# Small matmuls in another order, and pairs of feature tiles computed together, in a two-layer RWKV-7 / mLSTM trunk

## The chip, the cores and the metric

One core of one Trainium2 chip runs the whole program. The metric is the device time of one execution in microseconds (us); of several runs the median is taken. A profiled execution gives the rows shown below. TensorE is PE in these rows (PEld: its weight loads), VectorE is DVE, ScalarE is ACT, GpSimd is POOL, SyncE is SP.

## The reference, cut to what matters

Layer 0 mixes time with RWKV-7, layer 1 with a chunkwise mLSTM; each is followed by a SwiGLU FFN. Width 1024, 1024 frames, float32.

```python
r, wl, k, v, al, gl = outs                      # projections of token-shifted mixes
w_log = -softplus(-(w0 + tanh(wl) @ w2)) - 0.5  # "lora" of the decay; a = sigmoid(a0 + al @ a2)
state = state * w_t + (state @ a_t) b_t + v_t k_t   # per head 64 x 64, one step per frame
y = state @ r_t
...
w_intra = exp(d_log - m_t) * einsum('bhctd,bhcsd->bhcts', q, k)   # mLSTM scores
x = x + g1 * (mixed @ w_out);  x = x + g2 * swiglu(...)
```

## The kernel before, in words

Features lie on the partitions, frames on the free axis, in two halves (`hf`) of 512 frames. A **wide product** (`rkv` for r, k and v, `project` for w_out) makes eight feature tiles of 128 x 512. `dense` (line 244) makes one: for each of eight blocks `kt` of the input three matmuls, high weights by high input, high by low, low by high, all in one PSUM bank, 24 matmuls a tile. The weights of a tile come through `weights` (line 237): a load, an ACT copy to the high part (line 211) and a DVE subtraction to the low part (line 212). In the stage of the chunks (below) the tags `whi` and `wlo` have two buffers each and the PSUM tag `dn` two banks; where `self.deep` is set, c1 and c2 serve as well. `spill` (line 418) evicts a bank on ACT and stores it. The input parts come from `mixed` (line 403) into the 18 buffers of tag `a`.

The RWKV recurrence is solved in chunks of 64 frames. Each of 16 rounds (a pair of heads times a half) passes through four steps, one behind the other in a pipeline over the rounds (`chunks`, line 1450): `rw_prep` (masked score matrices), `rw_inverse` (inverse of a triangular 64 x 64 matrix per chunk and head, from 16 x 16 blocks up), `rw_solve`, and `rw_chain` with `rw_finish` (the state, chunk by chunk). Between the steps `run` lets a generator of **fillers** go on by a quota: the products v of the first half, the gate, the loras and k, r, v of the second half, the first out-projection. This is "the stage of the chunks" in what follows.

In `rw_inverse` (line 657) the first two groups of small matmuls are 16 x 16: 8 in each of four partition quadrants, quadrant after quadrant, with `tile_position=(32 * q, 32 * q)` (lines 697 to 709). The last groups are 32 x 32: for each end `e` of the partitions eight matmuls into bank `iv`, an ACT copy, eight more, another copy, and then the same for the other `e` (lines 719 to 729). In `rw_solve` (line 731) two groups of 16 matmuls of 64 x 64 go chunk by chunk, two heads in a row on the same partitions (lines 754 to 765), and a third goes through bank `tr` for one `e` and then the other (lines 769 to 776). A float32 matmul of these stands as two MATMUL instructions in the trace: 32 matmuls are 64 there. `ml_prep` (line 1284) forms the scores of two heads, four matmuls each over 64 partitions, head after head in two banks.

`lora` (line 428) ends with eight tiles of two matmuls: the first over 128 partitions (`st` holds the high weights on partitions 0 to 63 and the low ones on 64 to 127; `th` and `tl` are twice the same 64 rows), the second over partitions 0 to 63 alone (line 449).

The order on each engine is made by a planner from priorities and a model of times; a matmul that waits holds up those behind it on its engine. `ahead` raises the priority of a block.

Of the kernel before, what the change touches and what calls it, by code (L numbers as in the profile page):

```python
# [17 lines left out]
P = 128  # L18
D = 1024
T = 1024  # L20
KT = 8
# [108 lines left out]
class K:  # L130
# [113 lines left out]
    def dense(self, ps, w, xs, m=P):  # L244
# [3 lines left out]
        for kt, (xh, xl) in enumerate(xs):  # L248
# [2 lines left out]
            self.mm(ps, hi[:, c], xl, start=False, stop=False)  # L251
            self.mm(ps, lo[:, c], xh, start=False, stop=kt == n - 1)


    def ada_prep(self):
        nc = self.nc
# [171 lines left out]
    def lora(self, hf, arr, xs=None):  # L428


        nc, A = self.nc, self.A
        first, second, bias, seg, func = {"s": ("lw", "w2", "w0", 1, AF.Tanh), "a": ("la", "a2", "a0", 4, AF.Copy)}[arr]
        xs = xs or self.mixed(seg)
        ps = self.bank("dn")
        self.dense(ps, self.weights(A[first]), xs)
        yield 5
        t = self.t("tmp")
        nc.scalar.activation(t, ps, func)
        th, tl = self.a0()
        self.split(th, tl, t)  # L440
        raw, hi, st = self.wtiles(A[second])
        nc.scalar.activation(hi, raw, AF.Copy)
        nc.scalar.activation(st[0:64], raw[0:64], AF.Copy)
        nc.vector.tensor_tensor(st[64:128], raw[64:128], hi[64:128].bitcast(F32), SUB)
        for j in range(KT):
            c = slice(j * P, j * P + P)
            ps = self.bank("dn")
            self.mm(ps, st[:, c], th, start=True, stop=False)
            self.mm(ps, hi[0:64, c], tl[0:64], start=False, stop=True)
            self.spill(arr, j, hf, ps, AF.Sigmoid, bias=self.col(bias, j))  # L450
            if hf == 0 or j % 4 == 3:
                yield 2
# [37 lines left out]
    def rkv(self, hf, arr, xs=None):  # L490
        nc = self.nc
        seg, w = {"r": (0, "wr"), "k": (2, "wk"), "v": (3, "wv")}[arr]
        xs = xs or self.mixed(seg)
        if arr == "k":
            ss = self.t("ss", [16, HT])
        held = None

        def sums(j, sq):
            nonlocal p2
            if hf == 1 or j == 0:  # L500
                p2 = self.bank("iv" if hf == 0 else ("sc", "iv")[j % 2])
            sel = self.k_("hsel")[:, 14 - 2 * j:30 - 2 * j]
            if hf == 0:
                self.mm(p2[0:16], sel, sq, start=j == 0, stop=j == KT - 1)
            else:
                self.mm(p2[0:16], sel, sq)
            if j == 0 and hf == 1 or j == KT - 1 and hf == 0:
                nc.vector.tensor_copy(ss, p2[0:16])
            elif hf == 1:
                nc.vector.tensor_tensor(ss, ss, p2[0:16], ADD)  # L510

        p2 = None
        for j in range(KT):
            wt = self.early.pop(0) if self.early else self.weights(self.A[w][j])
            ps = self.bank("dn")
            self.dense(ps, wt, xs)
            if held:
                sums(*held)
            self.spill(arr, j, hf, ps)
            if arr == "k":  # L520
                sq = self.t("tmp")
                nc.scalar.activation(sq, ps, AF.Square, scale=self.col("k_k", j))
                held = j, sq
                if j == KT - 1:
                    sums(*held)
            if arr == "k" and j == KT - 1:
                self.kk_norm(ss, hf)
            self.done[arr, hf] = j + 1
            yield 6 if arr == "k" else 5

    def kk_norm(self, ss, hf):

# [124 lines left out]
    def rw_inverse(self, S):  # L657
# [36 lines left out]
        nc.vector.transpose(XN, XD)  # L694
        Y1 = self.t("Y1", [P, 8, 32])
        ps = self.bank("iv", [P, 8, 16])
        for q in range(4):
            r, e = slice(32 * q, 32 * q + 16), 0 if q >= 2 else 1
            o = 32 * (q % 2) + 16
            for c in range(8):  # L700
                self.mm(ps[r, c, :], SA[r, e, c, o:o + 16], XN[r, c, 0:16], tile_position=(32 * q, 32 * q))
        for q in range(4):
            r = slice(32 * q, 32 * q + 16)
            nc.scalar.activation(Y1[r, :, 0:16], ps[r], AF.Copy)
        ps = self.bank("iv", [P, 8, 16])
        for q in range(4):
            r = slice(32 * q, 32 * q + 16)
            for c in range(8):
                self.mm(ps[r, c, :], Y1[r, c, 0:16], XB[r, c, :], tile_position=(32 * q, 32 * q))
        for q in range(4):  # L710
            r = slice(32 * q, 32 * q + 16)
# [4 lines left out]
            o = 32 * (q % 2)  # L716
            nc.scalar.activation(SA[r, e, :, o:o + 32], XD[r], AF.Copy)
        Y1 = self.t("Y1", [P, 8, 32])
        for e in range(2):
            o = 0 if e else 64  # L720
            r0, r1 = slice(o, o + 32), slice(o + 32, o + 64)
            ps = self.bank("iv", [P, 8, 32])
            for c in range(8):
                self.mm(ps[r1, c, :], SA[r0, e, c, 32:64], XN[r0, c, :], tile_position=(o, o + 32))
            nc.scalar.activation(Y1[r1], ps[r1], AF.Copy)
            ps = self.bank("iv", [P, 8, 32])
            for c in range(8):
                self.mm(ps[r0, c, :], Y1[r1, c, :], XD[r1, c, :], tile_position=(o + 32, o))
            nc.scalar.activation(SA[r0, e, :, 32:64], ps[r0], AF.Copy)

    def rw_solve(self, S):

        nc = self.nc
        AR, SA = S["AR"], S["SA"]
        v = self.rload("v", S["j"], S["hf"])
        VU = self.t("VU", [P, 8, P])
        ps = self.bank("tr")
        for u in range(4):
            nc.tensor.transpose(ps[:, u * P:u * P + P], v[:, u * P:u * P + P], self.k_("ident"))
        p3 = ps.rearrange("p (u f) -> p u f", f=P)  # L740
        nc.scalar.activation(VU[0:64, 0::2, :], p3[0:64], AF.Copy)
        nc.scalar.activation(VU[64:128, 1::2, :], p3[64:128], AF.Copy)
        AT = self.t("AT", [P, 4, P])
        ps = self.bank("tr")
        fl = AR.rearrange("p c t -> p (c t)")
        for u in range(4):
            o = 2 * u * P + 64
            nc.tensor.transpose(ps[:, u * P:u * P + P], fl[:, o:o + P], self.k_("ident"))
        p3 = ps.rearrange("p (u f) -> p u f", f=P)
        nc.scalar.activation(AT[64:128], p3[0:64], AF.Copy)  # L750
        nc.scalar.activation(AT[0:64], p3[64:128], AF.Copy)
        Z = self.t("Z", [P, 4, P])
        ps = self.bank("px")
        for c in range(8):
            vr, ur = self.rows(c)
            for h in range(2):
                o = (c // 2) * P + 64 * h
                self.mm(ps[ur, o:o + 64], SA[vr, c % 2, 2 * (c // 2) + h, :], VU[vr, c, 64 * h:64 * h + 64])
        nc.scalar.activation(Z, ps.rearrange("p (u f) -> p u f", f=P), AF.Copy)
        ps = self.bank("px")  # L760
        for c in range(8):
            vr, ur = self.rows(c)
            for h in range(2):
                o = (c // 2) * P + 64 * h
                self.mm(ps[ur, o:o + 64], SA[ur, c % 2, 2 * (c // 2) + h, :], Z[ur, c // 2, 64 * h:64 * h + 64])
        p3 = ps.rearrange("p (u f) -> p u f", f=P)
        nc.scalar.activation(VU[64:128, 0::2, :], p3[64:128], AF.Copy)
        nc.scalar.activation(VU[0:64, 1::2, :], p3[0:64], AF.Copy)
        for e in range(2):
            ps = self.bank("tr", [P, 4, 64])  # L770
            ur = self.rows(e)[1]
            for u in range(4):
                for h in range(2):
                    hs = slice(64 * h, 64 * h + 64)
                    self.mm(ps[hs, u, :], AT[ur, u, hs], SA[ur, e, 2 * u + h, :])
            nc.vector.tensor_copy(AR[:, e::2, ur], ps)
        S["VU"] = VU

    def rw_chain(self, S):
# [48 lines left out]
    def project(self, y, w, l, xs, alloc, tag):  # L828
# [3 lines left out]
        for j in range(KT):  # L832
# [2 lines left out]
            hi, lo = alloc()  # L835
            self.split(hi, lo, t)
            parts.append((hi, lo))
        for n in range(KT):
            wt = self.weights(self.A[w][n])
            ps = self.bank("dn")  # L840
            self.dense(ps, wt, parts)
            nc.vector.scalar_tensor_tensor(xs[n], ps, self.mod[l][:, 16 + n:17 + n], xs[n], MUL, ADD)
            yield 5

# [437 lines left out]
    def ml_prep(self, pr, q, k, G):  # L1284
# [31 lines left out]
        for h in range(2):  # L1316
            w_ = dm[h].rearrange("p (c t) -> p c t", t=P)[:, :, P - 1:P]
            nc.vector.tensor_tensor(kw[:, :, 64 * h:64 * h + 64], p3[:, :, 64 * h:64 * h + 64],
                                    w_.to_broadcast([P, 4, 64]), MUL)
        for h in range(2):  # L1320
            hr = slice(64 * h, 64 * h + 64)
            ps = self.bank(self.alt("sc", "iv"))
            for c in range(4):
                cs = slice(c * P, c * P + P)
                self.mm(ps[:, cs], k[hr, cs], q[hr, cs])
            nc.vector.scalar_tensor_tensor(dm[h], ps, 0.125, dm[h], MUL, MUL)
        return dict(pr=pr, wi=wi, qw=qw, dm=dm, kw=kw, sc=sc)

    def ml_chain(self, S, va):
# [355 lines left out]
```

## Time and profile before

| | |
|---|---|
| median of 3 runs | 3062.93 us (3058.17 to 3084.75) |
| the profiled execution's own time | 3071.16 us, span 3069.2 us |
| PE, busy share of the span | 94% |
| DVE, ACT, POOL | 67%, 46%, 2% |
| mean granted clock of TensorE | 0.919 of full |

The page counts an engine as busy while at least one of its instructions runs. Matmuls are pipelined: a row's duration is not the time that it takes on the engine; the distance from its start to the next start is. A clock of 1.00 is 2.4 GHz, 0.50 is 1.2 GHz, and a mean between them tells how much of a stretch ran at each.

### The profile page before, as it was taken

The page shows a single profiled execution, that of the slowest core. Times are in us where ns is not written, and L with a number is a line of the kernel's source. Part 1 is how long each engine was busy: PE and PEld are TensorE (multiplying, and loading weights), DVE is VectorE, ACT ScalarE, POOL GpSimd, SP SyncE. Part 2 cuts the span into 40 slices and gives each one's busy share as a digit, 9 for nine tenths or more (in the row PEclk, how much of TensorE's full clock was granted, in tenths as well). Part 3 has the DMA queues.
Part 4 walks back from the last instruction along what each step waited for, and adds up shares of the span by engine and source line. Part 5 has one row for each costly group of instructions (what it writes and reads, how often), then busy time and mean ns, then how long its engine had stood idle before and what let it go on. Part 6 is the DMA issues. An engine that isn't in the chain of part 4 may idle for free.

```text
span 3069.2 us, 46769 instructions
## 1 busy us (share of the span) xinstructions
PE 2875.5 (94%) x17080; PEld 2254.1 (73%) x17080; DVE 2041.1 (67%) x4029; ACT 1409.5 (46%) x2641; POOL 73.5 (2%) x98
## 2 busy tenths in 40 slices
PE   6799989999989898999999998999989999999998
PEld 5577657677767677788877776777857788887776
DVE  7866665757666545978887758755555766667645
ACT  5756665656655554532224335322344533332532
POOL 0000000000000000000000000000010000000000
PEclk9899767979979689999999999988989999999999
DMA  8774433435354236466778854344545233336734
GB/s 289 258 236 141 111 98 92 116 101 142 102 155 125 80 95 210 151 191 220 239 243 281 270 178 157 115 124 151 158 134 168 93 117 103 103 114 229 256 120 149
DMA packets 359721, 492.38 MB, mean 160 GB/s; under 512 B 125212, under 2 KB 208796, under 8 KB 359492
## 3 DMA queue, kind: packets, MB, share of 16 engines
q1 hardware_dynamic: 345668, 464.24, 47.9%
q10 hardware_dynamic: 13824, 25.17, 2.2%
q8 instruction: 134, 2.20, 0.3%
q14 instruction: 95, 0.78, 0.1%
HBM read 359.77 MB, written 129.50 MB: 159 GB/s over the span
## 4 chain that ended last, share of the span: by engine, by line
PE 61%; DVE 13%; DMA 12%; issue 7%; ACT 5%; POOL 1%; SPq 1%; DVEq 0%; POOLq 0%; ACTq 0%
PE dn L207 23%; PE c L207 18%; PE iv L207 8%; PE px L207 6%; PE sc L207 4%; DMA tt<-gd 2%; DMA wraw<-in_wdn 2%; DMA wraw<-wsd 1%; DMA bgs<-in_ada 1%; DVE wq L212 1%; ACT wq L211 1%; DVE ga L212 1%; PE tr L207 1%; DMA bgs<-in_wdn 1%; DMA wsd<-bgs 1%
## 5 line engine op out<-in xcount | busy, mean ns | idle before, releaser
L207 PE MATMUL dn<-a,whi 128*128 128x512 f32 (+1 forms) x1224 | 473.2, 451 | 19.1 <-ACT a L211 7.8
L207 PE MATMUL c<-ga,wq 128*128 128x512 f32 x1446 | 355.6, 395 | 10.2 <-ACT ga L211 8.6
L211 ACT ACTIVATE wq<-wraw 128x1024 fp32r<-128x1024 f32 x202 | 210.7, 1057 | 330.9 <-DVE wraw L890 82.0
L207 PEld LDWEIGHTS c<-ga,wq 128*128 128x128 f32 x1446 | 271.9, 190 | 76.2 <-ACT ga L211 11.5
L207 PEld LDWEIGHTS dn<-a,whi 128*128 128x128 f32 (+1 forms) x1224 | 242.8, 206 | 89.4 <-issue 14.6
L212 DVE TENSOR_TENSOR wq<-wraw,wq 128x1024 fp32r<-128x1024 f32 x202 | 244.3, 1221 | 85.1 <-ACT wq L211 84.8
L207 PE MATMUL dn<-a,wlo 128*128 128x512 f32 (+2 forms) x640 | 284.1, 448 | 7.6 <-ACT tmp L420 3.0
L207 PE MATMUL c<-gb,wq 128*128 128x512 f32 x894 | 221.6, 399 | 7.6 <-DVE wq L212 6.9
L207 PEld LDWEIGHTS c<-gb,wq 128*128 128x128 f32 x894 | 169.5, 192 | 47.9 <-DVE wq L212 8.0
L207 PEld LDWEIGHTS dn<-a,wlo 128*128 128x128 f32 (+2 forms) x640 | 131.3, 206 | 40.2 <-issue 6.8
L211 ACT ACTIVATE whi<-wraw 128x1024 fp32r<-128x1024 f32 (+2 forms) x96 | 100.4, 1046 | 127.4 <-PE dn L207 104.1
L212 DVE TENSOR_TENSOR wlo<-wraw,whi 128x1024 fp32r<-128x1024 f32 (+2 forms) x96 | 116.1, 1209 | 48.4 <-ACT whi L211 41.3
L207 PE MATMUL iv<-ga,wq 128*128 128x512 f32 x552 | 136.0, 389 | 0.0
L207 PE MATMUL px<-ga,wq 128*128 128x512 f32 x528 | 128.6, 389 | 0.0
L207 PEld LDWEIGHTS iv<-ga,wq 128*128 128x128 f32 x552 | 103.6, 188 | 21.5
L211 ACT ACTIVATE w<-wraw 128x384 fp32r<-128x384 f32 (+1 forms) x100 | 56.7, 567 | 129.6 <-PE c L207 55.0
L207 PEld LDWEIGHTS px<-ga,wq 128*128 128x128 f32 x528 | 99.1, 188 | 20.7
L207 PE MATMUL dn<-gb,wq 128*128 128x512 f32 x426 | 104.7, 397 | 5.2 <-ACT gb L211 4.7
L207 PE MATMUL iv<-gb,wq 128*128 128x512 f32 x432 | 104.9, 390 | 0.0
L207 PEld LDWEIGHTS dn<-gb,wq 128*128 128x128 f32 x426 | 81.3, 192 | 24.5 <-ACT gb L211 5.6
L207 PEld LDWEIGHTS sc<-AR,KB 64*128 64x128 f32 x512 | 77.9, 226 | 28.5 <-issue 14.0
L207 PE MATMUL sc<-AR,KB 64*128 64x128 f32 x512 | 94.6, 331 | 3.9 <-DVE KB L612 3.2
(600 smaller groups left out, 5761.7 us busy)
## 6 DMA issues: line engine op xcount, KB each, us to landing
wraw<-in_wgu SPq DMA_DIRECT2D x110, 512.0 KB, 3.6
tt<-gd SPq DMA_DIRECT2D x154, 256.0 KB, 4.0
KT<-in_ada SPq DMA_DIRECT2D x40, 512.0 KB, 5.4
gd<-x SPq DMA_DIRECT2D x77, 256.0 KB, 2.1
gd<-tt SPq DMA_DIRECT2D x72, 256.0 KB, 2.2
wraw<-wsd SPq DMA_DIRECT2D x32, 512.0 KB, 4.5
bgs<-in_ada SPq DMA_DIRECT2D x96, 128.0 KB, 3.4
wraw<-in_wdn SPq DMA_DIRECT2D x24, 512.0 KB, 4.4
```

The lines of the kernel that those rows point to most:

```text
L207: return self.nc.tensor.matmul(out, lhsT, rhs, start=start, stop=stop, **kw)
L211: self.nc.scalar.activation(hi, src, AF.Copy)
L212: self.nc.vector.tensor_tensor(lo, src, hi.bitcast(F32), SUB)
```

## The change

Six edits, the arithmetic the same but for one: (1) the two 16 x 16 groups of `rw_inverse` go chunk by chunk with the four quadrants inside; (2) the 32 x 32 groups of both `e` share a bank and alternate, so that there are two groups of 16 matmuls in place of four of 8; (3) the 64 x 64 groups of `rw_solve` alternate `e`, and the third one takes banks `tr` and `px` at once; (4) the scores of `ml_prep` alternate heads; (5) the second matmul of a lora tile reads all 128 partitions (it adds the product of the two low parts); (6) `dense_two` makes two feature tiles at a time, the second three blocks behind the first, for tiles 0 and 1 and tiles 6 and 7 of `rkv` in the stage of the chunks, and for tiles 0 and 1 of `project`.

```diff
+    def dense_two(self, tiles, xs, lag=3):
+        n = len(xs)
+        for i in range(n + lag):
+            for kt, (ps, (hi, lo)) in zip((i, i - lag), tiles):
+                if 0 <= kt < n:
+                    xh, xl = xs[kt]
+                    c = slice(kt * P, kt * P + P)
+                    self.mm(ps, hi[:, c], xh, start=kt == 0, stop=False)
+                    self.mm(ps, hi[:, c], xl, start=False, stop=False)
+                    self.mm(ps, lo[:, c], xh, start=False, stop=kt == n - 1)
 # lora
-            self.mm(ps, hi[0:64, c], tl[0:64], start=False, stop=True)
+            self.mm(ps, st[:, c], tl, start=False, stop=True)
 # rkv
-        for j in range(KT):
-            wt = self.early.pop(0) if self.early else self.weights(self.A[w][j])
-            ps = self.bank("dn")
-            self.dense(ps, wt, xs)
+        two = ((0, 1), (2,), (3,), (4,), (5,), (6, 7)) if hf == 1 or arr == "v" else [(j,) for j in range(KT)]
+        for js in two:
+            wt = [self.early.pop(0) if self.early else self.weights(self.A[w][j]) for j in js]
+            banks = [self.bank("dn") for _ in js]
+            if len(js) == 2:
+                self.dense_two(list(zip(banks, wt)), xs)
+            else:
+                self.dense(banks[0], wt[0], xs)
...
+            yield len(js) * (6 if arr == "k" else 5)
 # rw_inverse
-        for q in range(4):
-            r, e = slice(32 * q, 32 * q + 16), 0 if q >= 2 else 1
-            o = 32 * (q % 2) + 16
-            for c in range(8):
+        for c in range(8):
+            for q in range(4):
+                r, e = slice(32 * q, 32 * q + 16), 0 if q >= 2 else 1
+                o = 32 * (q % 2) + 16
                 self.mm(ps[r, c, :], SA[r, e, c, o:o + 16], XN[r, c, 0:16], tile_position=(32 * q, 32 * q))
...
+        ends = [(e, o, slice(o, o + 32), slice(o + 32, o + 64)) for e, o in enumerate((64, 0))]
+        ps = self.bank("iv", [P, 8, 32])
+        for c in range(8):
+            for e, o, r0, r1 in ends:
                 self.mm(ps[r1, c, :], SA[r0, e, c, 32:64], XN[r0, c, :], tile_position=(o, o + 32))
+        for e, o, r0, r1 in ends:
             nc.scalar.activation(Y1[r1], ps[r1], AF.Copy)
...
 # rw_solve
+        pairs = [(2 * u + e, h, u * P + 64 * h, *self.rows(e)) for u in range(4) for h in range(2) for e in range(2)]
+        for c, h, o, vr, ur in pairs:
+            self.mm(ps[ur, o:o + 64], SA[vr, c % 2, 2 * (c // 2) + h, :], VU[vr, c, 64 * h:64 * h + 64])
...
+        ps = [self.bank(tag, [P, 4, 64]) for tag in ("tr", "px")]
+        for u in range(4):
+            for h in range(2):
+                hs = slice(64 * h, 64 * h + 64)
+                for e in range(2):
+                    ur = self.rows(e)[1]
+                    self.mm(ps[e][hs, u, :], AT[ur, u, hs], SA[ur, e, 2 * u + h, :])
         for e in range(2):
-            ps = self.bank("tr", [P, 4, 64])
...
+            nc.vector.tensor_copy(AR[:, e::2, self.rows(e)[1]], ps[e])
 # project: tiles (0, 1) by dense_two, 2 to 7 by dense
 # ml_prep
+        ps = [self.bank(tag) for tag in ("sc", "iv")]
+        for c in range(4):
+            cs = slice(c * P, c * P + P)
+            for h in range(2):
+                hr = slice(64 * h, 64 * h + 64)
+                self.mm(ps[h][:, cs], k[hr, cs], q[hr, cs])
```

## Rows read from the trace of the kernel before

**Rows 1.** Page, 40 slices of the span: granted TensorE clock in tenths.

```profile
PEclk9899767979979689999999999988989999999999
```

**Rows 2.** Stretches: length, then busy us (instructions) of PE, PEld, DVE, ACT, POOL; clock.

```profile
255.00:1130.00 875.00, 828.84 (x7809) 610.69 (x7808) 540.23 (x1389) 525.59 (x1234) 30.15 (x30) 0.81 0.40 112
...
1000.00:1130.00 130.00, 121.01 (x1091) 90.58 (x1092) 67.00 (x179) 68.81 (x176) 6.83 (x4) 0.71 0.29 84
...
1960.00:2320.00 360.00, 330.76 (x1791) 266.96 (x1790) 203.15 (x532) 123.58 (x285) 25.75 (x35) 0.91 0.46 145
```

**Rows 3.** Chain that ended last, 255 to 1130 us, shares by engine and line.

```profile
by line: PE dn L207 32.3%; PE c L207 12.4%; PE iv L207 11.0%; PE sc L207 9.6%; PE px L207 7.3%; PE tr L653 2.1%; PE tr L207 1.9%; POOL gv L812 1.5%; issue 1.4%; PE tr L739 1.0%; PE tr L818 1.0%; PE tr L748 0.9%; ACT gj L810 0.8%; ACT a L211
```

**Rows 4.** Groups of PE, 255 to 1130 us: count | busy us, mean ns | idle before, releasers.

```profile
L207 PE MATMUL dn<-a,whi 128*128 128x512 f32 x695 | 281.5, 463 | 8.0 <-DVE a L212 3.5 <-ACT a L211 1.8 <-ACT tmp L420 1.7
...
L207 PE MATMUL tr<-SA,AT 64*64 64x64 f32 x512 | 32.0, 251 | 5.2 <-DVE AR L776 3.7 <-ACT AT L751 1.5
L207 PE MATMUL px<-VU,SA 64*64 64x64 f32 x512 | 31.6, 248 | 0.1
L207 PE MATMUL iv<-XN,SA 32*32 32x32 f32 x512 | 30.1, 223 | 2.0 <-DVE X L677 1.2 <-DVE XN L713 0.8
L207 PE MATMUL iv<-XD,Y 32*32 32x32 f32 x512 | 29.8, 222 | 1.4 <-ACT Y L725 1.4
L207 PE MATMUL px<-Z,SA 64*64 64x64 f32 x512 | 26.5, 250 | 0.5 <-ACT SA L729 0.5
```

**Rows 5.** Timeline of PE, one 16 x 16 group: start, duration, operation, count.

```profile
622.10 1.52 PE L207 MATMUL iv<-XN,SA 16*16 16x16 f32 x64
623.55 0.50 PE L207 MATMUL dn<-a,wlo 128*128 128x512 f32 x1
623.89 0.62 PE L207 MATMUL dn<-a,whi 128*128 128x512 f32 x2
624.35 0.40 PE L207 MATMUL dn<-a,wlo 128*128 128x512 f32 x1
```

**Rows 6.** Timeline of PE, a 32 x 32 group at each clock level.

```profile
565.20 0.69 PE L207 MATMUL iv<-XD,Y 32*32 32x32 f32 x16
565.82 0.73 PE L207 MATMUL dn<-a,whi 128*128 128x512 f32 x2
...
636.20 1.06 PE L207 MATMUL iv<-XD,Y 32*32 32x32 f32 x16
637.19 0.80 PE L207 MATMUL c<-st,AR 128*128 128x128 f32 x2
```

**Rows 7.** Stretches of 0.01 us, readers of XN: PE busy (x matmuls in flight), clock.

```profile
273.36:273.37 0.01, 0.01 (x7) 1.00 0.07 6
273.55:273.56 0.01, 0.01 (x10) 1.00 0.34 32
```

**Rows 8.** Timeline of PE, two 64 x 64 groups on different partitions.

```profile
283.45 0.27 PE L207 MATMUL px<-Z,SA 64*64 64x64 f32 x1
283.47 0.27 PE L207 MATMUL tr<-SA,AT 64*64 64x64 f32 x1
```

**Rows 9.** Timeline of PE, the mLSTM scores of two heads, low clock.

```profile
2006.36 0.42 PE L207 MATMUL sc<-x,x 64*128 64x128 f32 x1
2006.54 0.42 PE L207 MATMUL iv<-x,x 64*128 64x128 f32 x1
2006.57 0.42 PE L207 MATMUL sc<-x,x 64*128 64x128 f32 x1
```

**Rows 10.** Timeline of PE, second matmuls of two lora tiles, first stage.

```profile
114.90 0.50 PE L207 MATMUL dn<-a,whi 64*128 64x512 f32 x1
...
115.76 0.50 PE L207 MATMUL dn<-a,whi 64*128 64x512 f32 x1
```

**Rows 11.** Groups of ACT and DVE, 255 to 1130 us: the split of the weights.

```profile
L211 ACT ACTIVATE whi<-wraw 128x1024 fp32r<-128x1024 f32 (+1 forms) x45 | 47.0, 1044 | 24.6 <-PE dn L207 24.6
...
L212 DVE TENSOR_TENSOR wlo<-wraw,whi 128x1024 fp32r<-128x1024 f32 (+1 forms) x45 | 54.4, 1208 | 11.0 <-ACT whi L211 7.0 <-PE dn L207 3.8
```

More of the change, by code (lines that the diff above doesn't have):

```diff
@@ L512, in rkv @@
         p2 = None
-        for j in range(KT):
-            wt = self.early.pop(0) if self.early else self.weights(self.A[w][j])
-            ps = self.bank("dn")
-            self.dense(ps, wt, xs)
[L517 to L524, printed above, removed]
-                    sums(*held)
[L526 to L529, printed above, removed]
+        two = ((0, 1), (2,), (3,), (4,), (5,), (6, 7)) if hf == 1 or arr == "v" else [(j,) for j in range(KT)]
[6 more added lines that the diff above has]
+                self.dense(banks[0], wt[0], xs)
+            for j, ps in zip(js, banks):
+                if held:
+                    sums(*held)
+                self.spill(arr, j, hf, ps)
+                if arr == "k":
+                    sq = self.t("tmp")
+                    nc.scalar.activation(sq, ps, AF.Square, scale=self.col("k_k", j))
+                    held = j, sq
+                    if j == KT - 1:
+                        sums(*held)
+                if arr == "k" and j == KT - 1:
+                    self.kk_norm(ss, hf)
+                self.done[arr, hf] = j + 1
+            yield len(js) * (6 if arr == "k" else 5)
     def kk_norm(self, ss, hf):
@@ L705, in rw_inverse @@
         ps = self.bank("iv", [P, 8, 16])
-        for q in range(4):
-            r = slice(32 * q, 32 * q + 16)
-            for c in range(8):
+        for c in range(8):
+            for q in range(4):
+                r = slice(32 * q, 32 * q + 16)
                 self.mm(ps[r, c, :], Y1[r, c, 0:16], XB[r, c, :], tile_position=(32 * q, 32 * q))
@@ L718, in rw_inverse @@
         Y1 = self.t("Y1", [P, 8, 32])
[L719 to L723, printed above, removed]
+        ends = [(e, o, slice(o, o + 32), slice(o + 32, o + 64)) for e, o in enumerate((64, 0))]
+        ps = self.bank("iv", [P, 8, 32])
+        for c in range(8):
+            for e, o, r0, r1 in ends:
                 self.mm(ps[r1, c, :], SA[r0, e, c, 32:64], XN[r0, c, :], tile_position=(o, o + 32))
+        for e, o, r0, r1 in ends:
             nc.scalar.activation(Y1[r1], ps[r1], AF.Copy)
-            ps = self.bank("iv", [P, 8, 32])
-            for c in range(8):
+        ps = self.bank("iv", [P, 8, 32])
+        for c in range(8):
+            for e, o, r0, r1 in ends:
                 self.mm(ps[r0, c, :], Y1[r1, c, :], XD[r1, c, :], tile_position=(o + 32, o))
+        for e, o, r0, r1 in ends:
             nc.scalar.activation(SA[r0, e, :, 32:64], ps[r0], AF.Copy)
@@ L753, in rw_solve @@
         ps = self.bank("px")
[L754 to L758, printed above, removed]
+        pairs = [(2 * u + e, h, u * P + 64 * h, *self.rows(e)) for u in range(4) for h in range(2) for e in range(2)]
+        for c, h, o, vr, ur in pairs:
+            self.mm(ps[ur, o:o + 64], SA[vr, c % 2, 2 * (c // 2) + h, :], VU[vr, c, 64 * h:64 * h + 64])
         nc.scalar.activation(Z, ps.rearrange("p (u f) -> p u f", f=P), AF.Copy)
         ps = self.bank("px")
[L761 to L765, printed above, removed]
+        for c, h, o, vr, ur in pairs:
+            self.mm(ps[ur, o:o + 64], SA[ur, c % 2, 2 * (c // 2) + h, :], Z[ur, c // 2, 64 * h:64 * h + 64])
         p3 = ps.rearrange("p (u f) -> p u f", f=P)
@@ L768, in rw_solve @@
         nc.scalar.activation(VU[0:64, 1::2, :], p3[0:64], AF.Copy)
-        for e in range(2):
-            ps = self.bank("tr", [P, 4, 64])
[L771 to L776, printed above, removed]
+        ps = [self.bank(tag, [P, 4, 64]) for tag in ("tr", "px")]
[5 more added lines that the diff above has]
+                    self.mm(ps[e][hs, u, :], AT[ur, u, hs], SA[ur, e, 2 * u + h, :])
+        for e in range(2):
+            nc.vector.tensor_copy(AR[:, e::2, self.rows(e)[1]], ps[e])
         S["VU"] = VU
@@ L837, in project @@
             parts.append((hi, lo))
[L838 to L843, printed above, removed]
+        for ns in ((0, 1), *((n,) for n in range(2, KT))):
+            wt = [self.weights(self.A[w][n]) for n in ns]
+            banks = [self.bank("dn") for _ in ns]
+            if len(ns) == 2:
+                self.dense_two(list(zip(banks, wt)), parts)
+            else:
+                self.dense(banks[0], wt[0], parts)
+            for n, ps in zip(ns, banks):
+                nc.vector.scalar_tensor_tensor(xs[n], ps, self.mod[l][:, 16 + n:17 + n], xs[n], MUL, ADD)
+                yield 5
     def parts(self, xs, tag):
@@ L1319, in ml_prep @@
                                     w_.to_broadcast([P, 4, 64]), MUL)
-        for h in range(2):
[L1321 to L1326, printed above, removed]
+        ps = [self.bank(tag) for tag in ("sc", "iv")]
[4 more added lines that the diff above has]
+                self.mm(ps[h][:, cs], k[hr, cs], q[hr, cs])
+        for h in range(2):
+            nc.vector.scalar_tensor_tensor(dm[h], ps[h], 0.125, dm[h], MUL, MUL)
         return dict(pr=pr, wi=wi, qw=qw, dm=dm, kw=kw, sc=sc)
```

## The prediction

> **What bounds the kernel now.** I read the stretches first. In the stage of the chunks, 255 to 1130 us, PE is busy 829 of 875 us and idle 46, DVE and ACT are busy about 62% and 60%, and the granted clock is 0.81 [rows 2]; the page's clock line has its low digits there and almost nowhere else [rows 1]. So PE bounds this stage, and much of it runs at 1.2 GHz: with a share s at half speed the clock is 1 - s/2, so s is 0.38. Then the chain of waits of this stage: its PE entries add up to 79.5% [rows 3]. A microsecond taken off PE should thus shorten the stage by about 0.8; the rest passes through DVE, ACT, POOL and loads. Last the groups of PE in this stage: what the change reorders are the rows of iv, px and tr [rows 4], 150 us busy, and another 46 us of 16 x 16 groups (priced below). The matmuls of the wide products wait only 8.0 us in their largest group [rows 4].
>
> **The sixteen-wide groups.** Each takes 622.10 to 623.55, 1.45 us, for 64 instructions, 22.7 ns each [rows 5]; two in each of 16 rounds make 46 us. Quadrants follow one another today, so two of them meet only at a border. Inside a quadrant 7 matmuls are in flight, at a border 10, in the same bank [rows 7]: the next quadrant starts while the last still works, and neither slows. Bounds for the new order: at 7/10 of the time, 1.02 us a group, saving 14 us; with all four quadrants at once a quarter of 1.34 plus 0.11 for the change of tiling, 0.44, saving 32. I take 0.65, between them, since a border shows only the beginning of an overlap of two: **26 us**.
>
> A rule of the Trainium skill speaks against this. "TensorEngine Tiling (Array Packing)", section Restrictions and Gotchas, says that different row tiles cannot access the same PSUM bank simultaneously; by it edits 1 and 2 would save nothing. The trace of before disagrees, with 10 in flight against 7 in bank iv. "TensorE: Matmul & The Clock Gate", section "Wait — 56ns, not 53.3ns?", gives a floor of about 25 ns from start to start; the 22.7 ns here, an average over four quadrants, is already below it.
>
> **The 32-wide groups.** One of 16 instructions takes 0.62 us at the high clock and 0.99 at the low [rows 6]. The 64 of them are busy 59.9 us [rows 4], 0.94 each; a group's last 0.07 us (0.69 against 0.62, [rows 6]) lies under its successor, so 0.87 is occupied. Afterwards there are 32 groups in which two ends of the partitions alternate. If both run at once, a group costs what it cost: 32 x 0.87 saved. If not, nothing. Two groups of 64 x 64 on different partitions start 0.02 us apart and go on together [rows 8], so I take **28 us**.
>
> **The solve.** The third group (tr, 32.0 us busy in 32 batches [rows 4], 0.93 occupied each by the same tail) becomes 16 batches with four partition and column combinations in two banks. Score matmuls of two heads, on different partitions into different banks, advance side by side in the rows of mLSTM, 0.18 us after one another against 0.21 for one head's step [rows 9]. Bounds 2 and 15 us; I take **14**. The first group (px from VU) costs 31.6 us, the second, of the same size and number, 26.5 [rows 4]; the change gives both one order, **5 us** off the first, bounds 0 and 8. The second I leave.
>
> **Changes of tiling.** A wide matmul right behind a small group takes 0.34 us to the next start, 0.23 otherwise (two in 0.46) [rows 5]. 32 groups of the inverse and 16 of the solve go: 48 x 0.11, **5 us**, bounds 0 (where groups already touch) and 10 at the low clock.
>
> **The loras.** Two tiles' second matmuls stand 0.86 us apart, 115.76 against 114.90, with one first matmul between [rows 10]; two full ones take 0.46 [rows 5]. Of 0.40 x 32 tiles, 13 us, half lies among the chunks (**6 us**) and half in the first stage, where I count half of 6, **3 us**, since that stage also waits for its loads.
>
> **The mLSTM scores.** Eight calls with 16 instructions; side by side, 8 of them cost nothing. One costs 0.21 us at the low clock [rows 9], half of it at the high; at a clock of 0.91 [rows 2] s is 0.18, the mean 0.13: 64 x 0.13 = 8 us, at the stage's PE share **6**. Bounds 0 and 9. It needs both banks free before it starts, so the DVE read of the scores' predecessor in the second bank comes to stand in front of the first head too.
>
> **The pairs.** These hold two weights and two `dn` banks, all there are. A pair runs 9 matmuls alone, 30 alternating, 9 alone; 9 x 0.23 is 2.0 us. Tile 1's weights enter the buffers of the tile before, needed 2.0 us after that tile ends; the next tile's enter those of tile 0, free 2.0 us ahead of need. Before, 24 x 0.23 = 5.5 us. The split takes 1.04 on ACT and 1.21 on DVE [rows 11], 2.25 us, and both queues are 60% full: behind the split on ACT stand the copies of inverse and solve, on DVE the adds of the state. With another 1.0 us for work in the queue, a squeeze can cost 1.25 us of PE if no chunk matmul stands there; nine pairs (four products twice, the projection once) have 18: 22 us at most. The other end is a gain of 8 us, the idle time ahead of wide matmuls [rows 4], when new input parts are taken up at half the pace. Chunk matmuls have the higher priority and stand in most of these places: I take **4 us lost**.
>
> **The sum.** Among the chunks 26 + 28 + 14 + 5 + 5 + 6 = 84 us of PE, at 0.8 that is 67. With 3 and 6 outside, less 4: 72 us. The profiled execution's 3071.2 less 72 is 2999; the median of the runs lies 8.2 us under that execution, so **2990 us**.
>
> **The rivals.**
> *The clock rises with it* (15%). Small matmuls at the low clock are the ones that shrink, wide ones fill more of each stretch. If the clock of the stage went from 0.81 to 0.88, s falls from 0.38 to 0.24; 0.14 x 800 us no longer at half speed returns 56 us: 2935. For it: the low clock stands where small matmuls crowd. Against: nothing shows what sets it.
> *Other engines take over* (14%). The inverse has its copies on ACT, the chain its adds on DVE; with 10% less PE work they rise to about 68% busy, and waits like those on AR and AT (5.2 us now, [rows 4]) grow. If only 0.4 of the 84 passes: 34 + 9 - 4 = 39, so 3024.
> *They do not run together* (8%). Edits 1 and 2 and the first two solve groups gain nothing beyond today's overlap, because one bank or the issue of instructions limits them: 14 + 5 + 6 = 25 among the chunks, 20 at 0.8, with 9 - 4: 25 us, 3038. Against it stand rows 7 and 8. The two skill sentences above would lead here.
> *The pairs starve* (2%): 18 more lost, 3008.
> *The clock falls* (5%), the case on the other side. The place is the stage of the chunks; if PE, with less to do, waits more between small matmuls, it may be granted 1.2 GHz longer. At a clock of 0.71, which the stretch 1000 to 1130 already has [rows 2], s is 0.58, 0.20 x 800 = 160 us more at half speed cost 80 us, and the gain is gone: that is where it decides. At 0.65, s is 0.70, 128 us lost: 3063 - 72 + 128 = 3119. Against: the same wide matmuls in less time.
>
> **Chances.** My forecast has 56%. A change of 1% (31 us) is about what a measurement of this kernel can tell. Faster by more: the forecast, the rising clock, the starving pairs, 8 of the 14 and 2 of the 8, 83%. Within 1%: the other 12. Slower: 5. The range goes from the rising clock, 2935, to just beyond the case of no overlap, 3040; it holds all but the falling clock and the tails.
>
> **What will show it.** In the profile after: the 16 x 16 groups at 0.4 to 0.9 us from start to next start; half as many 32-wide groups, still near 0.62; tr in 16 batches; lora tiles of two matmuls at 0.46; the stage of the chunks near 805 us with a clock of 0.81 or better; idle PE time ahead of dn for `whi`, `wlo` or tmp in excess of 12 us would show the squeezes. I am wrong if small groups keep their lengths, if the stage's idle time doubles from 46 us, or if its clock moves by more than 0.05.

## The result and the profile after

The changed kernel took **2976.53 us** (median of 4 runs, 2973.5 to 2988.24), the kernel before 3064.2 in the same comparison: a ratio of 0.9709 [0.9665, 0.9753], 88 us less. The forecast was 2990. The profiled executions are 94.7 us apart (spans 3069.2 and 2974.5), and that is the difference taken apart below.

The page of the changed kernel: busy time of the engines, and the granted clock in 40 slices. They answer to the table and to [rows 1].

```profile
PE 2758.5 (93%) x17080; PEld 2171.6 (73%) x17080; DVE 2036.5 (68%) x4029; ACT 1405.8 (47%) x2641; POOL 72.8 (2%) x98
PEclk9898679999789899999999998898989999999999
```

The low digits among the chunks are fewer. To compare like with like, the stage is taken from here on from its first px<-VU,SA to its last c<-VU,SR. First that stretch of the kernel before: length, busy us (instructions) of PE, PEld, DVE, ACT, POOL, clock, DMA share, GB/s.

```profile
266.30:1148.30 882.00, 835.72 (x7858) 614.54 (x7857) 538.84 (x1388) 524.10 (x1234) 30.04 (x29) 0.81 0.39 112
```

Then the changed kernel: that stage, and a hundredth of a microsecond inside a 16 x 16 group, as in [rows 7].

```profile
258.50:1049.20 790.70, 719.95 (x7859) 528.46 (x7859) 534.24 (x1384) 519.10 (x1234) 30.21 (x29) 0.88 0.44 125
...
613.80:613.81 0.01, 0.01 (x25) 0.01 (x10) 0.00 (x0) 0.00 (x0) 0.00 (x0) 1.00 8.47 410
```

The stage lost 91.3 us. PE is busy 115.8 us less and idle 70.8 us instead of 46.3; the number of instructions is the same and the clock rose from 0.81 to 0.88. In the middle of a 16 x 16 group 25 matmuls are in flight (19 to 28 in the other moments read), where there were 7 within a quadrant and 10 at a border.

The chain of waits of the changed kernel, 247 to 1031 us, shares by engine and line, against [rows 3]:

```profile
by line: PE dn L207 29.7%; PE c L207 11.6%; PE sc L207 9.9%; PE px L207 8.8%; PE iv L207 4.2%; issue 2.5%; POOL gv L828 2.4%; ACT SA L735 1.7%; PE tr L671 1.4%; DVE Y L693 1.2%; PE tr L207 1.2%; DVE X L695 1.2%; ACT Y L743 1.0%; PE tr L768 
```

iv fell from 11.0% to 4.2%. PE still ends most steps, but its entries add up to some 67% where they were 79.5%; what grew are small shares of ACT, DVE, POOL and of issue. The groups of PE in the stage, against [rows 4]: count | busy us, mean ns | idle before, releasers.

```profile
L207 PE MATMUL dn<-a,whi 128*128 128x512 f32 x705 | 264.2, 438 | 6.6 <-ACT a L211 4.0 <-ACT whi L211 1.2 <-DVE a L212 0.8
L207 PE MATMUL dn<-a,wlo 128*128 128x512 f32 x385 | 166.2, 443 | 3.9 <-ACT tmp L433 1.8 <-ACT a L211 1.3 <-DVE a L212 0.7
L207 PE MATMUL sc<-AR,KB 64*128 64x128 f32 x448 | 83.6, 331 | 10.6 <-DVE KB L630 4.5 <-DVE Y L693 3.3 <-DVE AR L631 1.3
...
L207 PE MATMUL px<-VU,SA 64*64 64x64 f32 x512 | 26.7, 231 | 0.0
...
L207 PE MATMUL tr<-SA,AT 64*64 64x64 f32 x256 | 16.5, 241 | 0.6 <-ACT AT L771 0.5
L207 PE MATMUL iv<-XD,Y 32*32 32x32 f32 x512 | 13.3, 209 | 6.9 <-ACT Y L743 6.9
...
L207 PE MATMUL iv<-XN,SA 32*32 32x32 f32 x512 | 13.1, 206 | 9.0 <-DVE X L695 3.0 <-DVE Y L693 3.0 <-DVE XN L731 2.9
...
L207 PE MATMUL px<-SA,AT 64*64 64x64 f32 x256 | 11.7, 230 | 0.8 <-ACT VU L783 0.7
```

Ahead of the wide products stands no new idle time (6.6 against 8.0 us, whi 1.2, tmp 1.8). It grew ahead of the 32-wide groups, 6.9 us on the copy Y where it was 1.4 and 9.0 on DVE where it was 2.0, and ahead of the scores, 10.6 where it was 3.8. Last the timeline of PE in the changed kernel (start, duration, operation, count), against [rows 5, 6, 9]; the distance to the next start is the time taken.

```profile
613.57 0.69 PE L207 MATMUL iv<-XN,SA 16*16 16x16 f32 x64
614.18 0.37 PE L207 MATMUL sc<-AR,KB 64*128 64x128 f32 x1
...
618.28 0.69 PE L207 MATMUL iv<-XN,SA 32*32 32x32 f32 x32
618.90 0.50 PE L207 MATMUL dn<-a,wlo 128*128 128x512 f32 x1
...
632.12 0.68 PE L207 MATMUL tr<-SA,AT 64*64 64x64 f32 x16
632.73 0.50 PE L207 MATMUL dn<-a,wlo 128*128 128x512 f32 x1
...
636.51 0.68 PE L207 MATMUL px<-SA,AT 64*64 64x64 f32 x16
637.12 0.50 PE L207 MATMUL dn<-a,whi 128*128 128x512 f32 x1
...
1970.76 1.14 PE L207 MATMUL iv<-x,x 64*128 64x128 f32 x8
1971.83 0.74 PE L207 MATMUL dn<-AR,whi 128*128 128x512 f32 x2
1972.50 1.16 PE L207 MATMUL sc<-x,x 64*128 64x128 f32 x8
```

A 16 x 16 group takes 0.61 us (before 1.45). A 32-wide group of 32 instructions takes the 0.62 us that 16 took. But the third group of the solve still stands as two batches of 16, in tr and, 4.4 us later, in px; and the mLSTM scores go head after head, with wide matmuls between, as in seven of the eight calls. Two edits were written, but the planner did not issue them so.

### The profile page after: what moved, and what is told of

It reads as the page before. It is cut to its first block, busy times and chain, and to the rows that moved or that the text cites. A ratio compares the mean times of both kernels' runs of the same rounds, so it can differ in the third digit from the quotient of the medians.

```text
span 2974.5 us, 46776 instructions
## 1 busy us (share of the span) xinstructions
PE 2758.5 (93%) x17080; PEld 2171.6 (73%) x17080; DVE 2036.5 (68%) x4029; ACT 1405.8 (47%) x2641; POOL 72.8 (2%) x98
## 4 chain that ended last, share of the span: by engine, by line
PE 61%; DVE 14%; DMA 10%; issue 7%; ACT 5%; POOL 1%; SPq 1%; DVEq 0%; POOLq 0%; ACTq 0%
PE dn L207 22%; PE c L207 19%; PE px L207 7%; PE iv L207 7%; PE sc L207 4%; DMA tt<-gd 2%; DMA bgs<-in_ada 2%; DMA wraw<-in_wdn 1%; DMA wraw<-wsd 1%; DVE wq L212 1%; ACT wq L211 1%; DVE ga L212 1%; POOL gv L828 1%; PE tr L207 1%; DVE wlo L212 1%
## 5 line engine op out<-in xcount | busy, mean ns | idle before, releaser
L207 PE MATMUL dn<-a,whi 128*128 128x512 f32 (+1 forms) x1200 | 433.4, 430 | 18.0 <-ACT a L211 9.9
L207 PEld LDWEIGHTS dn<-a,whi 128*128 128x128 f32 (+1 forms) x1200 | 227.6, 197 | 76.5 <-ACT a L211 12.4
L207 PE MATMUL sc<-AR,KB 64*128 64x128 f32 x512 | 92.8, 325 | 10.6 <-DVE KB L630 4.5
```

Source lines behind the costliest of these rows:

```text
L207: return self.nc.tensor.matmul(out, lhsT, rhs, start=start, stop=stop, **kw)
```

## The experiments

All are timed beside the kernel before; gains are counted from its median in the same comparison. The diffs are cut. Questions: which edits carry the gain; whether the overlap does it, or only a new order that the planner finds, or the halved number of groups; why two edits did nothing; what moved the clock.

**The two edits of the inverse alone** (edits 1 and 2):

```diff
-        for q in range(4):
...
-            for c in range(8):
+        for c in range(8):
+            for q in range(4):
...
-        for e in range(2):
...
+        for c in range(8):
+            for e, o, r0, r1 in ends:
...
```

> Only edits 1 and 2, the small matmuls of the inverse; everything else as before. Theory A (the inverse is the main part: the occupied time of its groups falls from 103 to about 45 us, and the granted clock of the chunk stage rises with it): 60 to 80 us faster, 16-wide groups at 0.62 us, 32-wide ones 32 of 0.62, clock of the stage at 0.85 or more. Rival B (the inverse gives only its own 58 us times 0.8, the clock rises through the loras and the pairs): 40 to 50 us faster, clock within 0.02 of 0.81.

Measured: 2982.71 us, 0.9718 [0.9674, 0.9762], 85 us less, above the 60 to 80 of theory A. Nearly the whole gain, and the stage at 0.88:

```profile
263.10:1053.30 790.20, 728.22 (x7860) 529.38 (x7860) 535.19 (x1388) 524.03 (x1236) 31.83 (x29) 0.88 0.44 125
```

**The pairs of feature tiles alone** (edit 6):

```diff
-        for j in range(KT):
...
+            if len(js) == 2:
+                self.dense_two(list(zip(banks, wt)), xs)
...
```

> Only edit 6, two feature tiles at a time; everything else as before. Theory A (the pairs neither starve nor feed PE): within 10 us of before, idle PE time of the chunk stage 40 to 55 us. Rival C (they feed it: the inputs of the next product are made in time): 15 to 30 us faster, idle time 30 us or less. Rival D (weights and banks run out): 10 to 20 us slower, more idle time ahead of dn.

Measured: 3048.36 us, 0.9935 [0.9911, 0.9959], 20 us less. None of the three theories fits: idle time in the stage is 855.30 - 807.37 = 47.9 us against 46.3, so the pairs neither starve nor feed PE, yet the stage is 27 us shorter. That came with a clock of 0.85.

```profile
266.50:1121.80 855.30, 807.37 (x7858) 595.66 (x7857) 537.66 (x1384) 521.82 (x1234) 30.56 (x29) 0.85 0.40 115
```

**The loras alone** (edit 5):

```diff
-            self.mm(ps, hi[0:64, c], tl[0:64], start=False, stop=True)
+            self.mm(ps, st[:, c], tl, start=False, stop=True)
```

> Only edit 5, the second lora matmul over 128 partitions; everything else as before. Theory A: 12 to 18 us faster, of it 8 in the first stage (the changed kernel starts the chunks 8 us earlier) and 4 to 10 among the chunks. Rival B (it also lifts the clock of the chunk stage): 25 us or more faster, stage clock 0.84 or more.

Measured: 3038.62 us, 0.9898 [0.986, 0.9935], 29 us less, where theory A has 12 to 18. In the profiled execution the stage begins at 257.3 instead of 266.3, so the first stage gave 9 us, and the stage itself, at the old clock, lost 16.7. But that execution is one of the slower ones (3050 us, mean clock 0.920 over the whole span); the two fastest, 3024 and 3031 us, stand at 0.929 and 0.928. So part of the 29 us seems to come with the clock, as in rival B.

```profile
257.30:1122.60 865.30, 822.81 (x7857) 611.41 (x7856) 537.43 (x1387) 522.87 (x1234) 29.86 (x29) 0.81 0.40 114
```

**All but the pairs** (edits 1 to 5):

```diff
-        two = ((0, 1), (2,), (3,), (4,), (5,), (6, 7)) if hf == 1 or arr == "v" else [(j,) for j in range(KT)]
-        for js in two:
...
+        for j in range(KT):
...
-        for ns in ((0, 1), *((n,) for n in range(2, KT))):
...
+        for n in range(KT):
...
```

> Edits 1 to 5, without the pairs. Theory A: within 10 us of the changed kernel, ratio to before 0.968 to 0.975. Rival C (pairs feed PE): ratio 0.976 to 0.985. Rival D (pairs starve PE): ratio 0.962 to 0.967.

Measured: 2975.96 us, 0.9697 [0.9665, 0.9729], the changed kernel's time. Beside the other edits the pairs add nothing that can be measured. The parts are not additive: 85, 20 and 29 us alone make 134, together 88.

**The 16 x 16 groups alone** (edit 1):

```diff
-        for q in range(4):
...
-            for c in range(8):
+        for c in range(8):
+            for q in range(4):
...
```

> Only edit 1, the 16-wide groups with the four quadrants inside. Theory A (alternation shortens a group from 1.45 to 0.62 us; the clock of the chunk stage follows the occupied time of small matmuls): 27 us less on PE, 25 to 40 us faster with the clock at 0.83 to 0.86. Rival E (the clock follows the 32-wide groups alone): 15 to 25 us faster, clock within 0.01 of 0.81.

Measured: 3022.42 us, 0.9846 [0.9821, 0.987], 47 us less, above both theories. Groups at 0.62 us.

```profile
267.20:1091.10 823.90, 769.46 (x7857) 559.15 (x7857) 538.78 (x1388) 522.67 (x1234) 29.64 (x29) 0.86 0.42 120
```

PE is busy 66 us less. The 16 x 16 groups themselves, by distances from start to start summed over the stage, fell by 27 (47.5 to 20.4). The rest is work that this edit leaves alone, at a clock of 0.86.

**The 32-wide groups alone** (edit 2):

```diff
-        for e in range(2):
...
-            ps = self.bank("iv", [P, 8, 32])
-            for c in range(8):
+        ps = self.bank("iv", [P, 8, 32])
+        for c in range(8):
+            for e, o, r0, r1 in ends:
...
```

> Only edit 2, the 32-wide groups: two groups of both partition ends, alternating. Theory A: 30 us less on PE, 30 to 50 us faster, clock 0.83 to 0.86. Rival E (this edit alone lifts the clock): 55 us or more faster, clock 0.87 or more.

Measured: 3015.46 us, 0.982 [0.9781, 0.9859], 54 us less; stage 817.4 us, clock 0.87; the 32-wide groups 55.6 to 25.3 us.

**Both ends in one bank, but one end after the other** (the diff is against the run above):

```diff
-        for c in range(8):
-            for e, o, r0, r1 in ends:
+        for e, o, r0, r1 in ends:
+            for c in range(8):
...
```

> The 32-wide groups of both ends in one bank as in edit 2, but end after end, not alternating: two trips to ACT in place of four, the matmuls as slow as before. Theory A (what counts is that both ends run at once): a group of 32 takes 1.1 us or more at the high clock and the kernel gains 10 us at most. Rival F (what counts is half the trips and tilings): within 15 us of the kernel with edit 2 whole.

Measured: 3030.88 us, 0.9871 [0.9855, 0.9886]. The stage, and one such group in the timeline of PE:

```profile
266.70:1109.50 842.80, 791.18 (x7860) 589.56 (x7860) 535.69 (x1388) 525.02 (x1236) 31.86 (x29) 0.85 0.41 117
...
632.93 1.09 PE L207 MATMUL iv<-XN,SA 32*32 32x32 f32 x32
633.95 0.50 PE L207 MATMUL dn<-a,whi 128*128 128x512 f32 x1
```

1.02 us for 32, where alternation takes 0.62: without it the ends overlap little, so alternation is what makes them run together. Yet even so 38 us are gained, where 10 at most were expected. The 32-wide groups themselves account for 12 of it (55.6 to 43.8): two groups of 16 had cost 2 x 0.62, and half the trips through the copy and half the changes of tiling are gone. The rest lies in other work, at the clock of 0.85 that the pairs alone had too, so how much of the 38 us is owed to the halved number of groups is not shown. Alternation adds some 15 us; the two intervals touch.

**The written order kept.** Since the planner had undone edits 3 (third group) and 4, here it is told to keep them:

```diff
-                    self.mm(ps[e][hs, u, :], AT[ur, u, hs], SA[ur, e, 2 * u + h, :])
+                    ins = self.mm(ps[e][hs, u, :], AT[ur, u, hs], SA[ur, e, 2 * u + h, :])
+                    if (u, h, e) != (0, 0, 0):
+                        self.tc.keep_in_program_order(ins)
...
-                self.mm(ps[h][:, cs], k[hr, cs], q[hr, cs])
+                ins = self.mm(ps[h][:, cs], k[hr, cs], q[hr, cs])
+                if (c, h) != (0, 0):
+                    self.tc.keep_in_program_order(ins)
```

> The changed kernel, with the planner bound to the written order inside two groups: the mLSTM scores (edit 4) and the third group of the solve (edit 3), which it had issued head after head and end after end. Theory A (the written alternation never reached PE): scores of a call in 0.95 us in place of 1.9, third group 16 batches of 0.6 us: 8 to 16 us faster than the changed kernel, ratio to before 0.963 to 0.968. Rival G (the wait for both banks costs what running together saves): ratio 0.970 to 0.975.

Measured: 2974.63 us, 0.9686 [0.9666, 0.9707], not apart from the changed kernel. The timeline shows both edits doing what they were meant to:

```profile
638.55 0.27 PE L207 MATMUL px<-SA,AT 64*64 64x64 f32 x1
638.56 0.27 PE L207 MATMUL tr<-SA,AT 64*64 64x64 f32 x1
...
639.17 0.50 PE L207 MATMUL dn<-a,whi 128*128 128x512 f32 x1
...
1872.84 0.37 PE L207 MATMUL sc<-x,x 64*128 64x128 f32 x1
1872.85 0.37 PE L207 MATMUL iv<-x,x 64*128 64x128 f32 x1
...
1873.93 0.74 PE L207 MATMUL dn<-KT,whi 128*128 128x512 f32 x2
```

The solve's 32 instructions take 0.62 us, the mLSTM's 16 take 1.09 where 8 took 1.07. The stretch from the first to the last of the mLSTM scores shortened from 308.6 to 301.2 us, and the third group's sum fell from 22.9 to 14.1. But the stage of the chunks, at a clock of 0.87, was 9 us longer in the profiled execution (2979.9 us, 5 above the median), and ate it:

```profile
256.70:1056.60 799.90, 735.41 (x7856) 529.92 (x7856) 539.25 (x1384) 520.23 (x1234) 29.68 (x29) 0.87 0.43 124
```

**Another order with no overlap.** The kernel before with quadrants and ends the other way round, so that the planner has a new order to work on and nothing else:

```diff
-        for q in range(4):
+        for q in (3, 2, 1, 0):
...
-        for e in range(2):
+        for e in (1, 0):
```

> The kernel before with the quadrants of the 16-wide groups taken from the last to the first, and the other end first in the 32-wide groups: the same instructions, groups and trips, only another order around them. Theory A (the clock of the chunk stage follows what the edits save): within 10 us of before, stage clock 0.80 to 0.825. Rival H (any other order of this stage moves it, and the gains of the pairs alone and the merged ends are of that kind): 15 us or more from before in either direction, clock 0.835 or more, or under 0.79.

Measured: 3068.3 us, 1.0003 [0.9984, 1.0022]. This new order moves nothing, so a new order as such does not bring the gain; it is the only one that was tried.

**The 16 x 16 groups three times over**, in the changed kernel, to bring the time of small matmuls back and see whether the clock follows:

```diff
-        for c in range(8):
+        for c in [*range(8)] * 3:
             for q in range(4):
...
```

> The changed kernel with every 16-wide group issued three times over, alternating: a group takes about 1.6 us again, as long as before the change, 33 us more on PE in all. Theory A (the clock follows the time that small matmuls occupy): clock of the chunk stage falls from 0.88 to about 0.86, 40 to 60 us slower than the changed kernel. Rival J (the clock follows the number of trips, tilings and waits, which stay as in the changed kernel): clock 0.87 to 0.885, 20 to 35 us slower.

Measured: 3074.28 us, 1.0012 [0.9986, 1.0039], 98 us above the changed kernel, with the clock back at 0.81. Inconclusive as to the clock, because something else came in. The stage, the costliest row of the waits of PE (us in total, times, longest), and the page's row of queue q8, which carries the program's instructions (packets, MB, share of 16 engines' span), first for this run, then for the changed kernel.

```profile
256.50:1157.40 900.90, 790.52 (x11952) 589.68 (x11952) 538.28 (x1384) 526.13 (x1236) 31.16 (x29) 0.81 0.39 110
...
PE iv L207 <- issue: 67.6, 34, 4.5
...
q8 instruction: 166, 2.72, 0.4%
...
q8 instruction: 135, 2.21, 0.3%
```

And the timeline in the stage's first groups, the idle time ahead in brackets:

```profile
269.06 0.41 PE L207 MATMUL iv<-XN,SA 16*16 16x16 f32 x32 [3.56 <-issue]
...
271.35 0.95 PE L207 MATMUL iv<-XB,Y 16*16 16x16 f32 x91
274.86 0.32 PE L207 MATMUL iv<-XB,Y 16*16 16x16 f32 x18 [2.56 <-issue]
```

PE stands still inside a group for microseconds, and the profile names no engine and no load that it waits for. But the trace shows packets of 16 KB on q8 from 266.02 to 267.53 and from 272.61 to 273.63, and PE goes on 1.53 and 1.23 us after they end. All 35 waits of this kind in the stage, 67.9 us, end 1.2 to 1.6 us after such a packet, so PE seems to have run out of program. With 4096 matmuls and 4096 weight loads more, 31 packets were added, some 62 bytes an instruction; a group of 192 matmuls and 192 loads is then more than one packet. The kernel before and the changed one have no such wait in the stage.

The stage is 110 us longer than the changed kernel's: PE is busy 71 us more, 40 of it in the 16 x 16 groups (20.3 to 60.7), and idle 40 us more, the 68 us of stalls having replaced some of the other waits. Whether the clock fell by the small matmuls or by the stalls cannot be told.

**The scores of the chunks as well.** The same step taken further: in the changed kernel the mLSTM scores are kept in their order (the third group of the solve is not), and the score matmuls of `rw_prep`, 80.6 us in the stage of the kernel before, alternate heads in two banks.

```diff
-                ps = self.bank("sc", [P, 4, P])
-                for q in range(4):
-                    self.mm(ps[:, q], KB[hs, 4 * u + q, :], AR[hs, 4 * u + q, :])
+            ps = [self.bank(tag, [P, 4, P]) for tag in ("sc", "iv")]
+            for q in range(4):
+                for h in range(2):
...
+                    ins = self.mm(ps[h][:, q], KB[hs, 4 * u + q, :], AR[hs, 4 * u + q, :])
+                    if (q, h) != (0, 0):
+                        self.tc.keep_in_program_order(ins)
...
```

> The changed kernel with the mLSTM scores kept in the written order, and the score matmuls of rw_prep treated likewise: two heads in banks sc and iv, alternating, in place of head after head in one bank. These score groups occupy 78 us among the chunks now. Theory A: half of it is saved, 30 us of PE at 0.8 and 7 us in the mLSTM: 25 to 40 us faster than the changed kernel, ratio to before 0.957 to 0.963. Rival K (bank iv, shared with the inverse, makes both wait, or other engines have become the bound): ratio 0.966 to 0.975, idle PE time among the chunks over 90 us.

Measured: 3159.81 us, 1.0288 [1.0261, 1.0315]. The waits of PE, 250 to 1240 us:

```profile
PE iv L207 <- DVE XN L715: 30.9, 8, 7.8
PE iv L207 <- ACT Y L725: 27.4, 8, 7.0
PE iv L207 <- DVE XN L734: 21.4, 15, 2.5
```

And its stage of the chunks:

```profile
279.40:1231.60 952.20, 727.88 (x7616) 523.62 (x7615) 526.93 (x1369) 511.76 (x1199) 27.67 (x29) 0.77 0.35 100
```

PE is idle 224 us where it was 71: the bank iv belongs to the inverse, whose steps hang on one another, and sharing it puts the scores into that chain. (The stretch begins behind the first round's inverse here and holds 240 matmuls fewer, so the busy times do not compare.) The clock is 0.77 with the most idle time.

**The same with another bank:**

```diff
-            ps = [self.bank(tag, [P, 4, P]) for tag in ("sc", "iv")]
+            ps = [self.bank(tag, [P, 4, P]) for tag in ("sc", "tr")]
```

> As the run with alternating rw_prep scores, the second head's in bank tr, which transposes use and the inverse does not, in place of iv. Theory K1 (bank iv was the cost: prep and inverse held each other up): the score groups stay at about 46 us, idle PE time among the chunks falls from 224 to under 100 us, 15 to 35 us faster than the changed kernel, ratio to before 0.957 to 0.966. Rival K2 (any second bank taken from this stage costs more than the alternation gives, since all eight are in use): idle time over 100 us, ratio over 0.975.

Measured: **2932.76 us** (5 runs, 2922.91 to 2946.78), 0.9574 [0.9549, 0.96]. This beats both kernels, the one before by 131 us and the changed one by some 44, of which some 9 lie in the mLSTM scores (308.6 to 299.1 us from the first to the last). Its stage of the chunks:

```profile
256.30:1010.90 754.60, 687.42 (x7864) 492.26 (x7864) 538.63 (x1388) 524.97 (x1240) 30.14 (x29) 0.90 0.46 132
```

And the groups of the scores in it, count | busy us, mean ns | idle before, releasers:

```profile
L207 PE MATMUL sc<-AR,KB 64*128 64x128 f32 x224 | 44.9, 330 | 5.8 <-DVE KB L630 4.4 <-DVE SR L651 1.1
...
L207 PE MATMUL tr<-AR,KB 64*128 64x128 f32 x224 | 42.7, 325 | 0.9 <-DVE SR L651 0.9
```

The two rows of busy time overlap: by distances from start to start the scores occupy 49 us, 78.5 in the changed kernel. Idle time is back at 67 us; only the bank differs from the run above.

## Why the prediction was right

The forecast of 2990 missed by 13 us, but not because every step held. The overlap of the inverse came as foretold; the steps of the solve, the mLSTM scores, the tilings and the loras gave less; and the clock, which the sum put at nothing, gave about as much as these fell short, and more. Step by step, with times in the stage summed from start to next start, idle time left out:

| step | foretold us | measured us |
|---|---|---|
| 16 x 16 groups | 26 | 27 (47.5 to 20.4) |
| 32-wide groups | 28 | 31 (55.6 to 24.9) |
| solve, third group | 14 | 4 (27.1 to 22.9) |
| solve, first group | 5 | 5 (28.5 to 23.5) |
| tilings and loras | 11 | in the next row |
| all other work of PE | 0 | 49, that row in it |
| **PE in the stage** | **84** | **116** |
| share that shortens the stage | 0.8 | 0.79 (91.3 of 115.8) |
| first stage | 3 | 8 |
| mLSTM scores | 6 | 0.6 |
| pairs | -4 | 0 (changed kernel against all but the pairs) |

The stages between the chunks and the mLSTM scores became 6 us longer (806.5 to 812.5), which no step foretold; the run with only another order has 817 there, so this stretch scatters by as much without any edit to it. What follows the scores is 1 us shorter.

**The overlap.** Right, in mechanism and size: 0.65 was taken, 0.61 measured, and two ends of the 32-wide groups take the 0.62 of one. "They do not run together" is excluded. By the rule of the Trainium skill on PSUM banks ("TensorEngine Tiling (Array Packing)", Restrictions and Gotchas) the four quadrants, as different row tiles, could not access bank iv together; it does not hold for these tiles, with 25 in flight. The floor of about 25 ns between starts that the Trainium skill gives ("TensorE: Matmul & The Clock Gate", "Wait — 56ns, not 53.3ns?") fits one quadrant, where the records of the kernel before lie 25 ns apart; across quadrants those of the changed kernel begin 6 to 7 ns apart.

**The planner.** The steps of the solve's third group and of the mLSTM scores failed: not in their price (with the order kept, 27.1 us became 14.1, and 7.4 us came off the mLSTM stretch) but because the written order is not the issued one. The third group's second bank, px, is held by the group of Z until later, so the planner sent one half ahead. The first group's 5 us are luck: in the run with edits 1 and 2 alone, which leaves the solve as it was, the first group fell to 24.8 us and the third to 24.1. So 3.7 of the 5 and 3.0 of the 4 us in the table came without edit 3.

**The share that passes.** 0.79 against 0.8 is closer than the method: the same ratio, what the stage lost over what PE lost in it, is 1.29 in the run with the loras alone and between 0.82 and 0.94 in the other faster runs. In the changed kernel the rest turned into waits on other engines, as "other engines take over" said in kind: idle time from 46.3 to 70.8 us, 5.5 of it on the copy Y behind the 32-wide groups.

**The clock.** The term that was missing. It rose from 0.81 to 0.88, more than the 0.05 that was named as making the prediction wrong, and rival one had priced just that move, at 56 us in all. In the records PE's time at 1.2 GHz fell from 315 to 167 us. On everything but the groups of inverse and solve it fell from 231 to 139 us while that work took 49 us less; half of these 92 us, 46, is an estimate of the clock's part, and an upper one (a 32-wide group takes 0.99 us at the low clock and 0.62 at the high [rows 6], less than twice as long). That leaves 3 us or a little more for the tilings and loras, where 11 were foretold. The same instruction shows it: dn from whi took 463 ns on average [rows 4], and 438 after. With the 7 us in the solve the clock gave PE about 50 us. That the sum still came out near is luck: nearly 30 us too much at the solve, the scores, the tilings and the loras stand against some 50 too little at the clock, of which 0.8 arrived, and the smaller errors of the table lie between.

What sets the clock stays open. Over the runs it goes up as the small groups shrink (0.86 and 0.87 for either edit, 0.88 for both, 0.90 with the scores) and down with idle time (0.77 at 224 us). But the pairs alone, with neither fewer small matmuls nor less idle time, ran at 0.85, and the run meant to separate these was spoilt by its stalls. Each of these figures is from one execution, and executions of one kernel differ: over the whole span, 52 of the kernel before had mean clocks from 0.911 to 0.925, four of the changed kernel 0.935 to 0.940.

## What to carry to other kernels

Matmuls that use a quarter or half of the array should be issued round robin over partition groups, even into one bank: here two ends took the 0.62 us of one, and four quadrants 0.61 us in place of 1.45. The wide work beside them ran at a higher clock afterwards, though why is not settled. Read the issued order in the trace afterwards, since a planner may undo the written one; and take the second bank from a chain that is not the critical one, for the same edit was worth 44 us with one bank and cost over 180 with another. Compare a step of the sum with a run that lacks that step before calling it right, since the clock moves all of them. In a sum, put a price on the clock for every stretch that has small matmuls at the low level.

## What the hardware showed unexpectedly

- Small matmuls in different quadrants start 6 to 7 ns apart and run together: 64 in 0.61 us. Two 64-row halves with two banks do as well, 16 of 64x128 in 1.09 us where 8 took 1.07.
- Groups of 192 tiny matmuls in a row, three times those of the changed kernel, met stalls of up to 4.5 us, 67.6 us in 34 places, each ending 1.2 to 1.6 us after a 16 KB packet of program code.
- Halving the number of small groups without overlapping them gave 38 us, 12 of it in these groups; alternation added some 15.
